# One 512-column matmul for the high weights, and weight sums made by accumulating DMAs, in a one-core streaming-encoder layer

## The chip, the cores and the metric

The kernel runs on 1 core of a Trainium2 chip. The metric is the device time of one execution in microseconds (us). Before the change three runs gave a median of 1380.38 us (1380.32 to 1382.34). The engines are named as in the profile: PE is TensorE's matmul, PEld its weight load, DVE is VectorE, ACT is ScalarE, POOL is GpSimd, and SP is SyncE, which here only issues DMAs.

## The reference

One layer over 512 positions and 2048 channels, everything in float32:

```python
hn = rmsnorm(x, norm_g)
proj = jnp.einsum('bsd,dc->bsc', hn, w_in)        # 2048 -> 6144 (q,k,v,gate of 3 branches) + 4 + 6144 merge gates
...
gates = jax.nn.sigmoid(proj[..., QKVG_COLS + N_HEADS:] + b_gate).reshape(b, s, N_BRANCH, D_MODEL)
...
ya = forgetting_attention(qa, ka, to_heads(br[:, :, 0, 2]), f_logit)
yb = chunked_relpos_attention(qb, kb, to_heads(br[:, :, 1, 2]), rel_bias)
yc = stick_breaking_attention(to_heads(br[:, :, 2, 0]), to_heads(br[:, :, 2, 1]), to_heads(br[:, :, 2, 2]))
ys = jnp.stack([from_heads(ya), from_heads(yb), from_heads(yc)], axis=2)
ys = ys * jax.nn.silu(br[:, :, :, 3])
up = jnp.einsum('bsnw,nwd->bsnd', ys, w_up)       # 512 -> 2048 for each branch
merged = jnp.sum(gates * up, axis=2)
return x + jnp.einsum('bsd,de->bse', merged, w_out)   # 2048 -> 2048
```

The two large products are the input projection and the output projection; the three attentions have four heads of 128 each.

## The kernel before, in words

**Float32 by three matmuls.** PE is fed in float32r, a rounded float32. So each operand is split into a high part and a low part: `split` lets ACT copy the source into a float32r tile (L239) and DVE subtract that from the source (L241). `mm3` (L245 to L249) adds three matmuls into one PSUM tile: high weights times high part (L247), high weights times low part (L248), low weights times high part (L249).

**Pairs by Strassen's scheme.** The positions are cut into halves of 256. Two blocks of 128 output columns, each with 2048 input channels in two halves of 1024, make one `PairTask`: a 2 by 2 product that is computed with seven block products instead of eight (in Winograd's form, with sums that are used again). One block product, a `Unit`, is 8 steps over 128 input channels, and each step is one `mm3` with 256 columns. The weights of a pair are four tiles `raw` of 128x1024 float32 (512 KB). Seven weight blocks are needed: the tiles of products 1, 2 and 4 as loaded, and four sums for products 5, 7, 6 and 3, which `sums` makes on DVE (L612, L616, L620, L625). The matching sums of the activations were made and split once (`x1`, `x2`, `t23`, `t4`, and `m...` for the output projection); a tile `Parts` holds high and low part of one half side by side, 128 x 2 x 2 x 256.

**Reading out.** A block product ends in the left 256 columns of a PSUM bank. `after_of` reads it out and adds the results up: in an ordinary pair the order of products is 1, 2, 6, 5, 7, 3, 4; products 6, 7 and 4 go on adding to the bank of product 1, and product 3 to that of product 5, so those banks are read while they are kept (ACT copies L673, L683, L689, L709; DVE adds L679, L693, L698). A pair that is built with `late=True` (two of 52: the first after the column stage, and the first of the output projection) uses another order and a fresh bank for each product, with more adds.

**What sets the order.** Everything is written as generators that a small planner (`Flow`) runs at build time. It keeps a clock for PE, ACT and DVE, gives each piece of work a cost and a due time, and writes the instructions of each engine in the order in which its model would start them. On the chip each queue then runs in that order and waits on semaphores. Weights are prepared two units ahead (`LA = 2`). Slots are counted: six `raw` tiles (`NR`), 21 tiles of 128x512 (`NT`, tag `t2`), 28 activation tiles (`NX`), and the PSUM banks of tag `acc`. Loads (`fetch`, L261) go through SP's queue, POOL has almost nothing to do.

**Stages.** Load and norm of x with the first head's columns (to about 100 us), then pairs for 11 further heads and for the merge gates with the attention of each head woven in between (to about 1078 us), then the up projections with 512-column matmuls (to about 1209 us), then eight pairs of the output projection.

Of the kernel before, what the change touches and what calls it, by code (L numbers as in the profile page):

```python
# [11 lines left out]
AF = mybir.ActivationFunctionType  # L12
# [149 lines left out]
def hybrid_kernel(  # L162
# [69 lines left out]

    def pair_of(name, dt=F32R):
        return t2(name + "h", dt), t2(name + "l", dt)
# [9 lines left out]

    def mm3(ps, lh, ll, rh, rl, start, stop, more=False):  # L245
# [3 lines left out]
        nc.tensor.matmul(ps, ll, rh, start=False, stop=stop, skip_group_check=more)  # L249

# [92 lines left out]
    class Unit:  # L343


        def __init__(self, mms, after=None, shape=(UK, P), srcs=(), room=0):
            self.shape, self.mms, self.after, self.srcs, self.room = list(shape), mms, after, srcs, room
            self.ready, self.raw, self.there = Event(), [], None

        def got(self, t, ev):  # L350
            self.raw.append((t, ev))

        def source(self):

            return self.raw[0]
# [7 lines left out]
    def load_unit(u):  # L363
        for s in u.srcs:
# [5 lines left out]
            u.got(t, fetch(to, s, flow.ready, 4 * u.shape[0] * P * P // 1024))  # L370
        for _ in range(u.room):
            yield raws, 1
            u.got(raw_tile(), None)
        if u.there is not None:
            u.there.t = 0.0

    def prep(u):
# [3 lines left out]
        if len(u.raw) < len(u.srcs) + u.room:  # L381
            u.there = Event()
            yield u.there
        src, ev = u.source()
        yield ev
        yield from split(u.hi, u.lo, src, n, u.ready)
# [105 lines left out]
    def combos(k):  # L492
# [8 lines left out]
        nc.vector.tensor_sub(a[:, LH], a[:, RH], a[:, LH])  # L501
# [3 lines left out]
        nc.vector.tensor_sub(b[:, RH], b[:, RH], a[:, LH])  # L505
        yield (DVE, q, *due)
        nc.vector.tensor_sub(b[:, LH], b[:, LH], b[:, RH])
# [20 lines left out]
    def strassen_ops(x1, x2, t23, t4):  # L528

        def part(ts, i):  # L530
            return lambda k: ts[k] and ts[k].half(i)

        return {1: part(x1, 0), 2: part(x2, 0), 3: part(x2, 1), 5: part(x1, 1), 6: part(t23, 0), 7: part(t23, 1),
                4: lambda k: t4[k // 2] and t4[k // 2].half(k % 2)}
# [28 lines left out]
    class Pair(Unit):  # L563


        def __init__(self, task, i, srcs=()):
            super().__init__(task.mms_of(i), task.after_of(i), srcs=srcs, room=1 if i == 0 else 0)
            self.task, self.p = task, task.order[i]

        def source(self):  # L570
            task = self.task
            if self.p == task.order[0]:
# [997 lines left out]
```

## Time and profile before

| what | before |
|---|---|
| median of 3 runs | 1380.38 us (1380.32 to 1382.34) |
| profiled execution | 1382.54 us, of which the span from first to last instruction is 1380.8 us |
| granted TensorE clock | 0.999 |
| DVE busy, ACT busy | 1100.3 us (80%), 772.3 us (56%) |
| data moved by DMA | 180.55 MB, mean 131 GB/s |

In the profile's groups each line gives the source line, the engine, the operation, output and inputs by the program's names, the shape and count, then busy time in us, the mean of one in ns, and the idle time of that engine just before these instructions. Matmuls overlap: one shows 280 ns, but the next starts 120 ns after it. So the pace of PE is read from the distance of two starts, not from the duration.

### The profile page before, as it was taken

The numbers are of one execution on the slowest core, as the hardware profiler recorded it, in microseconds if no ns is written. First come the engines' busy times: TensorE is split into PE (matmuls) and PEld (weight loads), VectorE is DVE, ScalarE is ACT, GpSimd is POOL, SyncE is SP. The second block draws the span as 40 slices with busy tenths as digits, with TensorE's granted clock in tenths as the row PEclk, the third lists the DMA queues.
The fourth block names the chain that finished last, engine by engine and source line by source line (L and its number), as shares of the span: only waits on it lengthen the run. The fifth ranks groups of instructions, "written<-read, shape, count | busy, mean of one in ns | idle before, by whom it ended". The sixth has DMA issues, their size and how long they took to land.

```text
span 1380.8 us, 25041 instructions
## 1 busy us (share of the span) xinstructions
PE 1363.8 (99%) x10306; PEld 1311.4 (95%) x10306; DVE 1100.3 (80%) x1488; ACT 772.3 (56%) x1233; POOL 4.4 (0%) x21
## 2 busy tenths in 40 slices
PE   7999999999999999999999999999999999989999
PEld 5789999999999999999999999999999888889998
DVE  5898987878878787787878869678687887897785
ACT  7546665646555566655667556555565755453433
POOL 0000000000000000000000000000000000000000
PEclk9999999999999999999999999999999999999999
DMA  9423333333343433434334242333425756434541
GB/s 340 152 90 111 104 100 115 96 126 121 94 123 107 131 122 94 123 113 131 116 100 123 92 143 95 108 115 108 128 80 184 278 187 193 142 94 170 177 140 63
DMA packets 68610, 180.55 MB, mean 131 GB/s; under 512 B 7672, under 2 KB 13944, under 8 KB 68496
## 3 DMA queue, kind: packets, MB, share of 16 engines
q1 hardware_dynamic: 64896, 174.69, 39.6%
q10 hardware_dynamic: 3600, 4.26, 0.9%
q8 instruction: 81, 1.33, 0.4%
q14 instruction: 33, 0.27, 0.1%
HBM read 159.24 MB, written 19.69 MB: 130 GB/s over the span
## 4 chain that ended last, share of the span: by engine, by line
PE 97%; DVE 2%; DMA 1%; issue 0%; ACT 0%; SPq 0%
PE acc L247 28%; PE acc L249 27%; PE acc L248 27%; PE att L248 3%; PE att L249 3%; PE att L247 3%; PE att L1042 1%; PE att L971 1%; DVE wl L241 1%; PE att L754 1%; PE att L1109 1%; PE att L1110 1%; PE att L1108 1%; DMA x<-in_xT 0%; PE att L1069 0%
## 5 line engine op out<-in xcount | busy, mean ns | idle before, releaser
L241 DVE TENSOR_TENSOR wl<-raw,wh 128x1024 fp32r<-128x1024 f32 (+1 forms) x412 | 493.7, 1200 | 192.1 <-ACT wh L239 191.0
L239 ACT ACTIVATE wh<-raw 128x1024 fp32r<-128x1024 f32 (+1 forms) x412 | 428.3, 1040 | 307.8 <-PE acc L248 201.1
L247 PE MATMUL acc<-x,wh 128*128 128x256 f32 (+1 forms) x1504 | 440.4, 293 | 9.1 <-ACT wh L239 9.1
L249 PE MATMUL acc<-x,wl 128*128 128x256 f32 (+1 forms) x1504 | 436.4, 290 | 0.1
L248 PE MATMUL acc<-x,wh 128*128 128x256 f32 (+1 forms) x1504 | 436.1, 290 | 0.0
L247 PEld LDWEIGHTS acc<-x,wh 128*128 128x128 f32 x1504 | 288.3, 192 | 15.4 <-ACT wh L239 9.1
L247 PE MATMUL acc<-t,wh 128*128 128x256 f32 x1056 | 301.2, 285 | 0.0
L249 PE MATMUL acc<-t,wl 128*128 128x256 f32 x1056 | 298.7, 283 | 0.0
L248 PE MATMUL acc<-t,wh 128*128 128x256 f32 x1056 | 298.7, 283 | 0.0
L248 PEld LDWEIGHTS acc<-x,wh 128*128 128x128 f32 x1504 | 288.2, 192 | 4.8 <-DVE wl L241 0.2
L249 PEld LDWEIGHTS acc<-x,wl 128*128 128x128 f32 x1504 | 287.9, 191 | 4.7 <-DVE wl L241 0.8
L247 PEld LDWEIGHTS acc<-t,wh 128*128 128x128 f32 x1056 | 202.4, 192 | 0.5
L248 PEld LDWEIGHTS acc<-t,wh 128*128 128x128 f32 x1056 | 202.4, 192 | 0.5
L249 PEld LDWEIGHTS acc<-t,wl 128*128 128x128 f32 x1056 | 202.3, 192 | 0.0
L248 PE MATMUL acc<-m,wh 128*128 128x256 f32 x448 | 127.8, 285 | 3.2 <-DVE m L241 3.2
L247 PE MATMUL acc<-m,wh 128*128 128x256 f32 x448 | 127.5, 285 | 0.8 <-ACT m L239 0.8
L249 PE MATMUL acc<-m,wl 128*128 128x256 f32 x448 | 127.6, 285 | 0.7 <-DVE wl L241 0.7
L248 PEld LDWEIGHTS acc<-m,wh 128*128 128x128 f32 x448 | 86.7, 193 | 3.8 <-DVE m L241 3.8
L247 PEld LDWEIGHTS acc<-m,wh 128*128 128x128 f32 x448 | 86.7, 194 | 1.0 <-ACT m L239 1.0
L249 PEld LDWEIGHTS acc<-m,wl 128*128 128x128 f32 x448 | 86.8, 194 | 0.9 <-DVE wl L241 0.9
L612 DVE TENSOR_TENSOR raw<-raw,raw 128x1024 f32<-128x1024 f32 x52 | 63.6, 1223 | 1.2
L625 DVE TENSOR_TENSOR raw<-raw,raw 128x1024 f32<-128x1024 f32 x52 | 63.4, 1220 | 0.6
(218 smaller groups left out, 1625.7 us busy)
## 6 DMA issues: line engine op xcount, KB each, us to landing
raw<-in_w_col SPq DMA_DIRECT2D x192, 512.0 KB, 3.6
raw<-in_w_out SPq DMA_DIRECT2D x32, 512.0 KB, 4.3
gl<-c SPq DMA_DIRECT2D x48, 256.0 KB, 2.0
raw<-in_w_up SPq DMA_DIRECT2D x32, 384.0 KB, 3.6
sg<-gl SPq DMA_DIRECT2D x48, 256.0 KB, 4.4
x<-in_xT SPq DMA_DIRECT2D x16, 256.0 KB, 6.2
xn<-in_xn SPq DMA_DIRECT2D x16, 256.0 KB, 6.2
xr<-in_xT SPq DMA_DIRECT2D x16, 256.0 KB, 4.3
```

Of the source, the lines that this page charges most:

```text
L239: nc.scalar.activation(hi, src, AF.Copy)
L241: nc.vector.tensor_sub(lo, src, f(hi))
L247: nc.tensor.matmul(ps, lh, rh, start=start, stop=False, skip_group_check=more)
L248: nc.tensor.matmul(ps, lh, rl, start=False, stop=False, skip_group_check=more)
L249: nc.tensor.matmul(ps, ll, rh, start=False, stop=stop, skip_group_check=more)
L612: nc.vector.tensor_add(w[5], w[7], w[4])
L625: nc.vector.tensor_sub(w[3], w[2], w[6])
L754: nc.tensor.matmul(two(first_ps[:2 * NH, :]), w2[:, kt, :], xs[kt].lo if j else xs[kt].hi, start=kt + j == 0, stop=kt + j == KT)
L971: nc.tensor.transpose(ps[:, blk(i)], self.p[i][:, blk(j)], identf)
L1042: nc.tensor.matmul(ps[:, i * P:], nu_r if i == j else nones_r, part, start=i == j and part is self.lk[j][0], stop=False)
L1108: nc.tensor.matmul(o, vh[:, blk(j)], h, start=j == 0, stop=False)
L1109: nc.tensor.matmul(o, vl[:, blk(j)], h, start=False, stop=False)
```

## The change

There are four parts.

- **mm2 for mm3 in the pairs.** One step of a block product becomes two matmuls: the high weights times high and low part together, 512 columns, into both halves of a PSUM bank; and the low weights times the high part, 256 columns, into the left half. The true result is the sum of the two halves.
- **Reading out.** Copies and adds now take all 512 columns, and where a result is final, `fold` adds the right half to the left. Where the sum of the blocks wants a minus sign, it folds with `minus`, which computes -a-b in one instruction. That goes with weight sums which are now plain additions: signs were moved from the weights to the activation sums (`combos`, `merged_a`, `merged_b`).
- **Weight sums.** `PairTask.load` loads five tiles instead of four; two of them (for products 5 and 7) get a second block added by an accumulating DMA that POOL issues (`add_up`), after the first one has landed. DVE makes the other two sums, in place.
- **Small ones.** `gates_of` starts its three loads together, the last product of the output pairs adds the residual in `c2_done`, and `merged_b` has a shorter due time.

```diff
+        def both(self, i):
+            return self.t[:, i, :, :], self.t[:, i, 0, :], self.ev[i]
...
+    def minus(to, a, b):
+        nc.vector.scalar_tensor_tensor(to, a, -1.0, b, op0=ALU.mult, op1=ALU.subtract)
...
+    def mm2(ps, lh, ll, r, rh, start, stop, more):
+        nc.tensor.matmul(two(ps), lh, r, start=start, stop=False, skip_group_check=more)
+        nc.tensor.matmul(ps[:, LH], ll, rh, start=False, stop=stop, skip_group_check=more)
...
+    def add_up(to, src, ready, kb):
+        nc.gpsimd.dma_start(to, src, accum_op=ALU.add)
+        line[1] = max(line[1], ready + 1.0) + kb / 170.0
+        return Event(line[1] + 2.5)
...
+        def load(self):
+            a11, a12, a21, a22 = self.src
+            for p, srcs in ((5, (a21, a22)), (1, (a11,)), (2, (a12,)), (7, (a11, a21)), (4, (a22,))):
+                yield raws, 1
+                t = self.w[p] = raw_tile()
+                ev = fetch(t, srcs[0], flow.ready, 512)
+                if len(srcs) > 1:
+                    ev = add_up(t, srcs[1], ev.t, 512)
+                self.there[p].t = ev.t
+            self.w[6], self.w[3] = self.w[1], self.w[2]
...
-            yield DVE, n
-            nc.vector.tensor_add(w[5], w[7], w[4])
-            set_(wev[5])
-            yield e1
-            yield DVE, n
-            nc.vector.tensor_sub(w[7], w[1], w[7])
-            set_(wev[7])
+            yield there[5]
             yield self.unit(1).ready
             yield DVE, n
-            nc.vector.tensor_sub(w[6], w[5], w[1])
+            nc.vector.tensor_add(w[1], w[1], w[5])
...
-            nc.vector.tensor_sub(w[3], w[2], w[6])
+            nc.vector.tensor_add(w[2], w[2], w[1])
...
-                    self.ps[p] = acc(bank)[:, LH]
+                    self.ps[p] = acc(bank)
...
-                    yield PE, mm_us(HS, 3)
-                    mm3(self.ps[p], u.hi[:, j, :], u.lo[:, j, :], rh, rl, j == 0 and not more, j == UK - 1, more)
+                    yield PE, mm_us(S) + mm_us(HS)
+                    mm2(self.ps[p], u.hi[:, j, :], u.lo[:, j, :], r, rh, j == 0 and not more, j == UK - 1, more)
...
+            def fold(to, src):
+                yield h
+                if p in (4, 7):
+                    minus(to, src[:, LH], src[:, RH])
+                else:
+                    add(to, src[:, LH], src[:, RH])
...
                 if p == 1:
+                    yield from new("u")
                     yield a
-                    nc.scalar.activation(self.u[:, LH], ps, AF.Copy)
+                    nc.scalar.activation(self.u, ps, AF.Copy)
...
                     elif p == 3:
                         yield ev[6]
                         yield v
-                        add(self.c1[:, RH], self.u[:, RH], ps)
+                        add(self.u, self.u, ps)
                         give(bank)
+                        yield from fold(self.c1[:, RH], self.u)
...
+                    else:
+                        yield lambda: hasattr(self, "c2")
+                        c = self.c2[:, LH]
+                        yield ACT, act_us(HS)
+                        nc.scalar.activation(c, ps[:, RH], AF.Copy, scale=-1.0)
+                        yield h
+                        nc.vector.tensor_sub(c, c, ps[:, LH])
                         give(bank)
```

What the change does to the order is seen at three places. On PE, in the middle of a pair, two steps of a block product stood like this before (`t` is the activation sum, `wh` and `wl` the high and low weights):

```order
L247 MATMUL acc_7720<-t_115_853,wh_7718 128x256
L248 MATMUL acc_7720<-t_115_853,wh_7718 128x256
L249 MATMUL acc_7720<-t_115_853,wl_7719 128x256
L247 MATMUL acc_7720<-t_118_870,wh_7718 128x256
L248 MATMUL acc_7720<-t_118_870,wh_7718 128x256
L249 MATMUL acc_7720<-t_118_870,wl_7719 128x256
```

and two steps with the change:

```order
L261 MATMUL acc_6473<-t_114_843,wh_6540 128x512
L262 MATMUL acc_6473<-t_114_843,wl_6541 128x256
L261 MATMUL acc_6473<-t_115_856,wh_6540 128x512
L262 MATMUL acc_6473<-t_115_856,wl_6541 128x256
```

Three rows became two; over the program PE has 2912 rows fewer, 52 pairs by 7 products by 8 steps.

On DVE, in the queue of an ordinary pair beside one head's attention, there stood before (`wl` is the low part of a weight block, `raw` a weight tile, `c` the read-out results, `al` an attention tile):

```order
L679 TENSOR_TENSOR c_6221<-c_6183,acc_6186 128x256
L241 TENSOR_TENSOR wl_6223<-raw_6174,wh_6222 128x1024
L241 TENSOR_TENSOR wl_6258<-raw_6244,wh_6257 128x1024
L241 TENSOR_TENSOR al_6256<-att_6268,ah_6255 128x512
L241 TENSOR_TENSOR wl_6298<-raw_5943,wh_6297 128x1024
L612 TENSOR_TENSOR raw_6281<-raw_6174,raw_6209 128x1024
L693 TENSOR_TENSOR c_6294<-c_6294,acc_6141 128x256
L616 TENSOR_TENSOR raw_6174<-raw_6049,raw_6174 128x1024
L241 TENSOR_TENSOR wl_6338<-raw_6049,wh_6337 128x1024
L241 TENSOR_TENSOR al_6296<-att_6308,ah_6295 128x384
L698 TENSOR_TENSOR c_6221<-c_6183,acc_6259 128x256
L620 TENSOR_TENSOR raw_6049<-raw_6281,raw_6049 128x1024
```

and at the same place of a pair with the change:

```order
L714 TENSOR_TENSOR u_5228<-u_5228,acc_5231 128x512
L690 TENSOR_TENSOR c_901_5265<-u_5228 128x256
...
L245 TENSOR_TENSOR wl_5322<-raw_5084,wh_5321 128x1024
L245 TENSOR_TENSOR al_5320<-att_5329,ah_5319 128x384
L726 TENSOR_TENSOR v_5318<-v_5318,acc_5195 128x512
L251 SCALAR_TENSOR_TENSOR c_922_5363<-v_5318 128x256
L245 TENSOR_TENSOR wl_5355<-raw_5222,wh_5354 128x1024
L245 TENSOR_TENSOR vl_5370<-att_5364,vh_5369 128x512
L633 TENSOR_TENSOR raw_5222<-raw_5222,raw_5118 128x1024
L735 TENSOR_TENSOR u_5228<-u_5228,acc_5290 128x512
```

The sums L612 and L616 are gone from the queue; each add from PSUM is twice as wide, and a fold of 256 columns stands behind it.

On SP, the loads of one pair and a bit (each row one 512 KB tile) with the change are the five in the middle of these rows:

```order
L274 DMA raw_4928<-in_w_col 128x1024
L274 DMA raw_5018<-in_w_col 128x1024
L274 DMA raw_5035<-in_w_col 128x1024
L274 DMA raw_5059<-in_w_col 128x1024
L274 DMA raw_5084<-in_w_col 128x1024
L274 DMA raw_5118<-in_w_col 128x1024
```

and POOL's queue, where no DMA stood before, has for the same tiles:

```order
L278 DMA raw_4928<-in_w_col 128x1024
L278 DMA raw_5059<-in_w_col 128x1024
L278 DMA raw_5118<-in_w_col 128x1024
```

A pair takes its tiles in the order product 5, 1, 2, 7, 4, so `raw_4928` and `raw_5059` are the accumulated tiles of one pair, and `raw_5118` is the first of the next.

More of the change, by code (lines that the diff above doesn't have):

```diff
@@ L363, in load_unit @@
     def load_unit(u):
+        if isinstance(u, Pair):
+            if u is u.task.units[0]:
+                yield from u.task.load()
+            return
         for s in u.srcs:
@@ L369, in load_unit @@
                 to = t.rearrange("p (c k) m -> p c k m", c=s.shape[1])
[L370 to L375, printed above, removed]
+            u.raw = t
+            u.there.t = fetch(to, s, flow.ready, 4 * u.shape[0] * P * P // 1024).t
     def prep(u):
@@ L380, in prep @@
         u.lo = wp.tile([P] + u.shape, F32R, tag="wl", name=nm("wl"), bufs=LA + 1)
[L381 to L386, printed above, removed]
+        yield u.source_there()
+        yield from split(u.hi, u.lo, u.source(), n, u.ready)
         u.split_done()
@@ L627, in sums, with free @@
-            yield self.unit(6).ready
+            nc.vector.tensor_add(w[2], w[2], w[1])
+            set_(there[3])
+            spawn(self.free(6), 1.0)
+        def free(self, p):
+            yield self.unit(p).ready
             give(raws)
```

166 lines of the change are left out of this document (83 added, 83 removed).

## The prediction

> **What bounds the kernel now.** I read the page's busy times, its chain that ended last, then PE's waits, then PE's starts one by one.
>
> ```profile
> span 1380.8 us, 25041 instructions
> PE 97%; DVE 2%; DMA 1%; issue 0%; ACT 0%; SPq 0%
> ...
> PE acc L247 <- ACT wh L239: 9.1, 1, 9.1
> PE acc L248 <- DVE m L241: 3.2, 3, 2.2
> PE acc L247 <- ACT m L239: 0.8, 1, 0.8
> PE acc L249 <- DVE wl L241: 0.7, 1, 0.7
> ```
>
> The chain is 97% PE. The last four rows are all of PE's waits (engine and line, what it waited for: us in total, times, longest): 9.1 us once at the start, and 4.7 us where the output projection begins. In between PE never waits. So the time is the number of matmuls by their pace, and only PE's own work, or a new wait of PE, can move it. The pace is read from starts (first column, us), where the widths meet:
>
> ```profile
> 403.67 0.28 PE L248 MATMUL acc<-x,wh 128*128 128x256 f32 x1
> 403.79 0.28 PE L249 MATMUL acc<-x,wl 128*128 128x256 f32 x1
> 403.91 0.40 PE L869 MATMUL att<-sqh,ones_r 128*128 128x512 f32 x1
> 404.14 0.39 PE L870 MATMUL att<-sql,ones_r 128*128 128x512 f32 x1
> 404.37 0.28 PE L247 MATMUL acc<-x,wh 128*128 128x256 f32 x1
> 404.49 0.28 PE L248 MATMUL acc<-x,wh 128*128 128x256 f32 x1
> ...
> 1109.66 0.39 PE L248 MATMUL att<-y,wh 128*128 128x512 f32 x1
> ...
> 1111.02 0.39 PE L248 MATMUL acc<-y,wh 128*128 128x512 f32 x1
> ```
>
> 256 columns take 0.12 us (403.67, 403.79, 403.91; 404.37, 404.49). 512 columns take 0.2267 us: from 1109.66 to 1111.02 there are six, 1.36 / 6. Twice the columns cost 0.1067 us more, so each matmul pays 0.2267 - 2 x 0.1067 = 0.0133 us whatever its width. The rows at 403.79 to 404.49 show that a change of width costs nothing on top, neither from 256 to 512 nor back: each has the distance of its own width.
>
> **The change part by part: PE.** A step was three matmuls of 256, 0.360 us. It becomes one of 512 and one of 256, 0.2267 + 0.1200 = 0.3467 us. The columns streamed are the same; one fixed part of 0.0133 us is saved. There are 52 pairs x 7 products x 8 steps = 2912 steps, and the two orders differ by that many PE rows: 2912 x 0.01333 = 38.8 us off the path.
>
> The Trainium skill, "TensorE: Matmul & The Clock Gate", section "Back-to-back issue gap", has the gap of single matmuls at N/2.4 + 2.5 ns when warm, and says that this leaves out the weight load. By its 2.5 ns the 2912 matmuls would be worth an estimated 7.3 us; the 13.3 ns of the rows, where every matmul loads weights, says 38.8.
>
> **Reading out and weight sums.** Durations by shape, from DVE's and ACT's groups (last columns: busy us, mean ns):
>
> ```profile
> L612 DVE TENSOR_TENSOR raw<-raw,raw 128x1024 f32<-128x1024 f32 x52 | 63.6, 1223 | 1.2
> L1342 DVE TENSOR_TENSOR sg<-att,sg 128x512 f32<-128x512 f32 x32 | 22.0, 687 | 13.0 <-PE att L249 13.0
> L698 DVE TENSOR_TENSOR c<-c,acc 128x256 f32<-128x256 f32 x50 | 20.8, 415 | 2.8 <-PE acc L249 2.2
> L441 DVE SCALAR_TENSOR_TENSOR rs<-rw,rt 128x512 f32<-128x512 f32 x16 | 11.1, 692 | 0.6
> ...
> L673 ACT ACTIVATE c<-acc 128x256 f32<-128x256 f32 x52 | 19.8, 381 | 29.0 <-PE acc L249 24.4 <-DMA out<-c 3.7
> L239 ACT ACTIVATE vh<-att 128x512 fp32r<-128x512 f32 x12 | 7.0, 582 | 0.0
> ```
>
> An ordinary pair on DVE: before, four sums of 1.22 and three adds of 0.415, 6.13 us. After, two sums, three adds of 512 columns at 0.687, and four steps of 256 (three folds, and one subtraction for product 4) at 0.42, 6.18 us. The instruction that `minus` uses has no price of its own: at 512 columns it takes 692 ns in L441, as a plain tensor-tensor does, so I take it as equal. ACT: before four copies of 0.38, 1.53 us; after three of 0.58 and one of 0.38, 2.13 us. So DVE stays even, and ACT gets 0.6 us per pair. Whether that hides is seen in the stretch of pairs:
>
> ```profile
> 200.00:1000.00 800.00, 800.00 (x6580) 794.79 (x6579) 631.33 (x799) 459.86 (x730) 1.57 (x3) 1.00 0.37 114
> ...
> L247 PE MATMUL acc<-x,wh 128*128 128x256 f32 x1172 | 334.3, 285 | 0.0
> L239 ACT ACTIVATE wh<-raw 128x1024 fp32r<-128x1024 f32 x256 | 270.3, 1056 | 158.6 <-PE acc L248 144.8 <-DVE raw L620 9.3 <-issue 4.4
> L247 PE MATMUL acc<-t,wh 128*128 128x256 f32 x873 | 248.9, 285 | 0.0
> ...
> 100.00:200.00 100.00, 100.00 (x788) 97.98 (x787) 89.07 (x146) 60.29 (x105) 0.00 (x0) 1.00 0.32 101
> 130.00:140.00 10.00, 10.00 (x82) 9.87 (x82) 9.80 (x18) 7.53 (x13) 0.00 (x0) 1.00 0.42 132
> ```
>
> The rows with a colon are window, length, then busy PE, PEld, DVE, ACT, POOL, then clock, DMA share and GB/s. In 800 us PE is busy throughout; (1172 + 873) / 56 = 36.5 pairs make 21.9 us a pair, with DVE 17.3 and ACT 12.6 us. With the change a pair lasts 21.9 - 0.75 = 21.17 us, with DVE 17.35 (82% for 79%) and ACT 13.2 us (62% for 57%). Between 130 and 140 us DVE is busy 98% and PE loses nothing: weights prepared two units ahead bridge it. So I cost this at nothing. Its cover is one product: where a product adds on to a bank that is still to be read out (6 on 1, 7 on 6, 3 on 5, 4 on 7), exactly one other product, 8 x 0.3467 = 2.77 us, stands between. The read-out takes 0.58 on ACT or 0.69 on DVE, and may stand behind a weight instruction of 1.06 (L239) or 1.22 us (L612's shape): 1.6 to 1.9 us. If that cover fails, PE waits, and the weights behind it in the two queues get late next.
>
> **The accumulating DMAs.** Nothing in the trace accumulates, so the cost is bounded by plain loads.
>
> ```profile
> raw<-in_w_col SPq DMA_DIRECT2D x192, 512.0 KB, 3.6
> q1 hardware_dynamic: 64896, 174.69, 39.6%
> ```
>
> A 512 KB load lands 3.6 us after its issue. By the stretch above, where 114 GB/s keep the 16 engines busy for 37%, 0.524 MB use 4.6 x 0.37 = 1.70 us of all sixteen (the whole program's 174.69 MB at 39.6% say 1.64). A pair has 8.1 us of such DMA time now. It gets one plain load more, 1.7, and two accumulates. The lower end is a plain load each, 1.7, in all 13.2 of 21.17 us (62%). The upper end is where the engines are full: (21.17 - 9.8) / 2 = 5.7 us each, 3.3 times a load. I take twice, 3.4 us each, as an accumulate also has to read the tile that it adds to: 78%. Latency is covered better still: with six slots a pair's tile for product 7 gets its slot when the pair before has split its own, one whole pair ahead, so 21 us for a load of 3.6 and the accumulate, and that for product 5 more. On SP the fifth load stands before the next pair's; SP waits there for slots that DVE frees, not for POOL. POOL's rows wait only for the first load and the slot. Three memsets of `forget_sums` stand among them in POOL's queue, and the planner puts these where their tiles come free. So nothing on the path; from 5.7 us on each further microsecond costs 104 of them.
>
> **Start of the output projection and end.** PE's waits on `m` there (3.2 us, L241) stand in DVE's queue behind this:
>
> ```profile
> 1199.57 1.22 DVE L612 TENSOR_TENSOR raw<-raw,raw 128x1024 f32<-128x1024 f32 x1
> 1201.36 1.22 DVE L616 TENSOR_TENSOR raw<-raw,raw 128x1024 f32<-128x1024 f32 x1
> ...
> 1377.60 0.42 DVE L705 TENSOR_TENSOR c<-xr,acc 128x256 f32<-128x256 f32 x1 [1.73 <-PE acc L249]
> ```
>
> Two sums of 1.22 us leave the queue just ahead of the splits that PE waits for, so up to 2.4 us come back; wider adds of the late pair (0.27 each) take some of it. I take 2.0, with bounds of 3.2 (all that wait) and 0. At the end one DVE instruction (L705) lay between the last matmul and the last store. With the change it is an ACT copy of 0.38, a subtraction and an add of 0.42 each: 0.8 us more, with no cover.
>
> **The sum.** The profiled execution took 1382.5 us for its span of 1380.8. 1382.5 - 38.8 - 2.0 + 0.8 = 1342.5. The median of the three runs is 2.2 us below that execution, so 1340.3. The hot stretch between 100 and 200 us, where DVE is 89% busy, holds the other late pair: seven adds that are 0.27 us wider and four folds of 0.42, against two sums of 1.22 less, 1.1 us more. It may cost a wait of that size at most, and I add most of it: 1341.
>
> **The rivals.**
>
> *The read-out becomes a wait.* If each pair loses once what ACT's and DVE's read-out have grown by together (0.2 + 0.27, say 0.4 us), 52 x 0.4 = 21 us come back: 1362. For it: DVE's share rises to 82%, and the extra tiles `u`, `v` at full width take `t2` slots for longer. Against it: no wait today in 1000 us, with 2.77 us of cover.
>
> *The accumulates fill the DMA engines: slower.* At four times a plain load, 6.8 us each, a pair needs 8.1 + 1.7 + 13.6 = 23.4 us of DMA time for 21.17 us of PE. PE then waits 2.2 us per pair for product 5's or 7's weights, 52 x 2.2 = 116 us: 1457. It decides from 3.3 times on, and makes the kernel slower from 3.6 times (0.75 us per pair). For it: nothing here shows how fast the engines add. Against it: 37% busy now, 21 us of lead.
>
> *The fixed part is not saved.* If a step of 512 and 256 cost nearly its old 0.360 us, because the 13.3 ns belonged to the columns or the load of weights and not to the instruction, only the page's 2.5 ns a matmul would be left: 1380.4 - 7.3 - 1.2 = 1372. Against it stand the starts at 403.79 to 404.49.
>
> **How the numbers follow.** The forecast, 1336 to 1348, gets 0.67; read-out waits (1348 to 1376) 0.20; the unsaved fixed part 0.03; DMA engines full 0.10. The range runs from 1336 (all 4.7 us of waits gone at the start of the output projection, no wait in the hot stretch, and 2 us for the spread between runs) to 1365, which takes in about three quarters of the read-out rival: 0.67 + 0.15 = 0.82. A difference under 0.2%, 2.8 us, can't be told from no change. Faster by more than that: the forecast, read-out waits and the unsaved fixed part, less 0.02 for waits that happen to eat it all: 0.88. Within it 0.02. Slower 0.10.
>
> **What would show it.** PE: some 7394 matmuls instead of 10306, starts in a pair 0.227 and 0.120 us apart, and PE's list of waits still without any on `u`, `v` or `raw` between 100 and 1070 us. DVE near 1104 us busy, ACT near 806 (34 more). DMA's share in the stretch of pairs about 0.78; POOL's DMAs landing in 4 to 8 us. The prediction is wrong if a step takes 0.36 us, if PE waits for an ACT or DVE read-out once per pair, or if the accumulates take over 5.7 us of the DMA engines each.

## The result, and the profile after

The median fell from 1380.35 us (4 runs, 1380.07 to 1382.34) to 1358.22 us (4 runs, 1357.42 to 1359.96): a ratio of 0.9838, 95% interval 0.9821 to 0.9855. The change saves 22 us, where 39 were forecast. The direction was right. The time lies inside the stated range, 1336 to 1365, but outside the forecast's own part of it, 1336 to 1348: the point, 1341, is 17 us too low.

The page of the changed kernel, its DMA queues, PE's list of waits, and the stretch of pairs between 200 and 1000 us (columns as in the prediction):

```profile
span 1356.7 us, 19802 instructions
PE 1336.8 (99%) x7394; PEld 1154.0 (85%) x7394; DVE 1106.6 (82%) x1592; ACT 803.6 (59%) x1240; POOL 94.2 (7%) x125
...
q0 software_dynamic: 14976, 54.53, 23.9%
...
raw<-in_w_col SPq DMA_DIRECT2D x236, 512.0 KB, 4.2
raw<-in_w_col POOLq DMA_DIRECT2D x88, 512.0 KB, 6.3
```

```profile
PE acc L255 <- ACT wh L243: 9.9, 1, 9.9
PE acc L261 <- DVE m L245: 4.0, 1, 4.0
PE att L256 <- DVE y L245: 1.0, 1, 1.0
PE acc L262 <- DVE wl L245: 0.8, 2, 0.5
```

```profile
200.00:1000.00 800.00, 800.00 (x4641) 700.80 (x4640) 651.24 (x890) 492.00 (x747) 65.42 (x77) 1.00 0.71 189
```

The number of matmuls, DVE's and ACT's busy time and the DMA share are near what was forecast (7394 matmuls, 1104 and 806 us, and a share of 0.78, where 0.71 was measured). PE is busy all 800 us and never waits there for a read-out or a sum. So what is missing in this stretch is missing in PE's own pace. Its starts, in the stretch of pairs:

```profile
499.36 0.40 PE L261 MATMUL acc<-x,wh 128*128 128x512 f32 x1
499.59 0.28 PE L262 MATMUL acc<-x,wl 128*128 128x256 f32 x1
499.71 0.40 PE L261 MATMUL acc<-x,wh 128*128 128x512 f32 x1
499.95 0.28 PE L262 MATMUL acc<-x,wl 128*128 128x256 f32 x1
...
502.19 0.40 PE L261 MATMUL acc<-x,wh 128*128 128x512 f32 x1
```

From 499.36 to 502.19 lie eight steps: 2.83 / 8 = 0.354 us, not 0.3467. The mean over all steps of pairs without an interruption (2464 steps; starts of the trace, gaps of over 25 ns left out) is 233.9 ns for 512 and 116.6 for 256, 350.6 together. By stages, each from the start of its first matmul to that of the next stage's:

| stage | before | after | difference | forecast |
|---|---|---|---|---|
| pairs up to the up projection | 969.9 | 947.5 | -22.3 | -32.0 (with the hot stretch) |
| up projection | 130.6 | 132.3 | +1.7 | 0 |
| first pair of the output projection | 26.6 | 27.5 | +0.9 | -2.75 |
| its seven other pairs | 142.0 | 137.0 | -5.0 | -5.2 |
| last matmul to the end | 3.55 | 4.31 | +0.8 | +0.8 |

Three rows are short: pairs by 9.7, the up projection by 1.7, the start of the output projection by 3.6. The other 2 us of the 17 are the step from the profiled execution to the median: it was 2.2 us before, and is 0.2 now.

### The profile page after: what moved, and what is told of

Same layout as the page of the kernel before. It is cut to its first block, busy times and chain, and to the rows that moved or that the text cites. A ratio compares the mean times of both kernels' runs of the same rounds, so it can differ in the third digit from the quotient of the medians.

```text
span 1356.7 us, 19802 instructions
## 1 busy us (share of the span) xinstructions
PE 1336.8 (99%) x7394; PEld 1154.0 (85%) x7394; DVE 1106.6 (82%) x1592; ACT 803.6 (59%) x1240; POOL 94.2 (7%) x125
## 3 DMA queue, kind: packets, MB, share of 16 engines
q0 software_dynamic: 14976, 54.53, 23.9%
## 4 chain that ended last, share of the span: by engine, by line
PE 96%; DVE 2%; DMA 1%; ACT 0%; issue 0%; SPq 0%; ACTq 0%; DVEq 0%
PE acc L261 49%; PE acc L262 25%; PE att L256 3%; PE att L257 3%; PE att L255 3%; PE acc L257 3%; PE acc L256 3%; PE acc L255 3%; DVE wl L245 1%; PE att L1088 1%; PE att L1017 1%; PE att L1156 1%; PE att L1155 1%; PE att L800 1%; DVE m L245 1%; PE att L1154 1%
## 5 line engine op out<-in xcount | busy, mean ns | idle before, releaser
L261 PE MATMUL acc<-x,wh 128*128 128x512 f32 x1408 | 505.8, 398 | 0.0
L262 PE MATMUL acc<-x,wl 128*128 128x256 f32 x1408 | 394.1, 280 | 0.0
L261 PE MATMUL acc<-t,wh 128*128 128x512 f32 x1056 | 381.0, 398 | 0.0
L261 PEld LDWEIGHTS acc<-x,wh 128*128 128x128 f32 x1408 | 264.5, 188 | 60.9
L261 PEld LDWEIGHTS acc<-t,wh 128*128 128x128 f32 x1056 | 198.4, 188 | 45.3
L261 PE MATMUL acc<-m,wh 128*128 128x512 f32 x448 | 158.8, 397 | 4.0 <-DVE m L245 4.0
L278 POOL DMA_DIRECT2D raw<-in_w_col x88 | 76.1, 864 | 943.1 <-DMA raw<-in_w_col 515.5
L261 PEld LDWEIGHTS acc<-m,wh 128*128 128x128 f32 x448 | 85.1, 190 | 23.6 <-DVE m L245 4.3
L722 ACT ACTIVATE u<-acc 128x512 f32<-128x512 f32 x50 | 29.8, 596 | 56.9 <-PE acc L262 56.9
L699 ACT ACTIVATE u<-acc 128x512 f32<-128x512 f32 x52 | 30.9, 593 | 41.0 <-PE acc L262 37.1
L256 PE MATMUL att<-y,wh 128*128 128x512 f32 x128 | 50.0, 391 | 1.1 <-DVE y L245 1.0
```

What stands on the lines that cost most here:

```text
L256: nc.tensor.matmul(ps, lh, rl, start=False, stop=False, skip_group_check=more)
L261: nc.tensor.matmul(two(ps), lh, r, start=start, stop=False, skip_group_check=more)
L262: nc.tensor.matmul(ps[:, LH], ll, rh, start=False, stop=stop, skip_group_check=more)
L278: nc.gpsimd.dma_start(to, src, accum_op=ALU.add)
L699: nc.scalar.activation(self.u, ps, AF.Copy)
```

## The experiments

Eleven kernels ran, in three lots. Ratios are to the kernel before, run beside them (1380.17, 1380.38 and 1380.59 us in the three lots).

**Which part is worth what: the merged matmul taken apart.**

```diff
-        nc.tensor.matmul(two(ps), lh, r, start=start, stop=False, skip_group_check=more)
+        nc.tensor.matmul(ps[:, LH], lh, rh, start=start, stop=False, skip_group_check=more)
+        nc.tensor.matmul(ps[:, RH], lh, r[:, 1, :], start=False, stop=False, skip_group_check=more)
```

> The wide read-out, the accumulating DMAs and everything else of the change, but the 512-column matmul taken apart again into two of 256 (high weights times high part into the left half, times low part into the right half). It measures what the merged matmul alone is worth. Theory A: PE's starts are 0.120 apart throughout as before, a step 0.360, so 2912 x (0.360 - 0.3503) = 28 us more than the changed kernel: 1386, that is some 6 us above the kernel before, the price of the other parts (start of the output projection, end). Theory B (DMA traffic slows PE): starts in the pairs over 0.120, step over 0.363, 1395 or more. If the other parts of the change bring nothing and cost nothing: 1380.

Measured: 1382.72 us, ratio 1.0019 (1.0009 to 1.0028). Its steps are 120 ns per matmul again. So all the other parts together, wide read-outs, folds and accumulating DMAs, cost 2.5 us (1382.72 - 1380.17), and the merged matmul alone brings 24.5 us (1382.72 - 1358.22): 8.4 ns per step, not 13.3. So most of the missing part belongs to the merged matmul, not to its surroundings.

**Do the accumulating DMAs slow PE down?** The 104 accumulating DMAs were left out, so the weights of products 5 and 7 lack their second tile.

```diff
-                if len(srcs) > 1:
-                    ev = add_up(t, srcs[1], ev.t, 512)
```

> The changed kernel without its 104 accumulating DMAs: the second block of the weight sums for products 5 and 7 is left out, so the output is not the reference's; loads, DVE, ACT and PE are as in the changed kernel. Theory A: PE's pace in the pairs is unchanged (0.350 per step), 1357 to 1358. Theory B: the pace returns to 0.3467 and the time to 1348. If the accumulates delay the start of the output projection or the up projections, one to three us come back there and nothing in the pairs.

Measured: 1359.58 us, ratio 0.9844 (0.983 to 0.9859), the same as the change. The stretch of pairs:

```profile
200.00:1000.00 800.00, 800.00 (x4639) 700.67 (x4638) 651.26 (x890) 492.18 (x747) 1.57 (x3) 1.00 0.46 140
```

4639 matmuls in 800 us for 4641: not one is bought by leaving them out, although the DMA share falls from 0.71 to 0.46. So contention of the DMAs with PE is out. The fall also prices the accumulate: 0.25 x 800 / 74 = 2.7 us of all sixteen engines each (77 of POOL's instructions less three memsets); by the queue's share it is 0.239 x 1356.7 / 104 = 3.1.

**The order of widths: grouped and folded.** In the first kernel a product does eight matmuls of 512, then eight of 256; in the second the order inside every other step is turned round, 512, 256, 256, 512.

```diff
-                    yield PE, mm_us(S) + mm_us(HS)
-                    mm2(self.ps[p], u.hi[:, j, :], u.lo[:, j, :], r, rh, j == 0 and not more, j == UK - 1, more)
+                    yield PE, mm_us(S)
+                    nc.tensor.matmul(two(self.ps[p]), u.hi[:, j, :], r, start=j == 0 and not more, stop=False,
+                                     skip_group_check=more)
+                for j in range(UK):
+                    r, rh, ev = self.ops[p](j)
+                    yield PE, mm_us(HS)
+                    nc.tensor.matmul(self.ps[p][:, LH], u.lo[:, j, :], rh, start=False, stop=j == UK - 1,
+                                     skip_group_check=more)
```

```diff
-                    mm2(self.ps[p], u.hi[:, j, :], u.lo[:, j, :], r, rh, j == 0 and not more, j == UK - 1, more)
+                    for i in ((0, 1) if j % 2 == 0 else (1, 0)):
+                        if i == 0:
+                            nc.tensor.matmul(two(self.ps[p]), u.hi[:, j, :], r, start=j == 0 and not more,
+                                             stop=j == UK - 1, skip_group_check=more)
+                        else:
+                            nc.tensor.matmul(self.ps[p][:, LH], u.lo[:, j, :], rh, start=False, stop=False,
+                                             skip_group_check=more)
```

> Each block product issues its eight 512-column matmuls first and then its eight 256-column ones; the same matmuls, columns and DMAs, but two changes of width per product instead of sixteen. Theory A (the lost part of the gain is the price of alternating widths: in the changed kernel a 512 is followed by a 256 after 0.230 to 0.241 us and that by a 512 after 0.112 to 0.120, 0.3503 us per step in the mean where 0.3467 was expected, some 10 us over the pairs): 512s 0.227 apart, 256s 0.120 apart, the stretch from the first pair to the first up projection 937 us instead of 947.5, total 1348. Theory B (the accumulating DMAs and the higher DMA traffic slow PE's reads): no change, 1358. Theory C (waits for the read-out of PSUM): no change or a little worse, 1358 to 1362.

> Steps in the order 512, 256, 256, 512, 512, 256, 256, 512: half the changes of width. Theory A by dose: half of the 10 us comes back, 1353. If the loss hangs on the rhythm of one 512 and one 256 and not on the number of changes, all of it comes back, 1348. Theories B and C: 1358.

Measured: grouped 1356.15 us (0.9824, 0.9808 to 0.9841), folded 1352.55 us (0.9797, 0.9782 to 0.9812). A step of pairs takes 349.5 and 348.7 ns, for 350.6 in the change. The order of widths matters, with the same instructions; but rows of eight of one width still don't reach 346.7. Within its rows of eight, the grouped kernel's 512s were 230 to 231 ns apart on average, where the up projection has 226.7. One difference was left that could explain it: a pair's operand of 512 is one run of 512 numbers, the up projection reads two runs of 256.

**The operand's layout.** The tiles of the pair operands were laid out as the up projection's, and in a second kernel the up projection's as the pairs' were.

```diff
-            self.hi, self.lo = self.t[:, :, 0, :], self.t[:, :, 1, :]
+            self.v = self.t if apart else self.t.rearrange("p h l s -> p l h s")
+            self.hi, self.lo = self.v[:, 0, :, :], self.v[:, 1, :, :]
...
-            return self.t[:, i, :, :], self.t[:, i, 0, :], self.ev[i]
+            return self.v[:, :, i, :], self.v[:, 0, i, :], self.ev[i]
```

> The tiles of pair operands are laid out with all high halves ahead of all low halves, so that the 512-column operand of a step is two runs of 256 numbers, as the up projection's was before; the y tiles keep their old layout, and the column sums, which read a high or a low half of a whole row, now read 512 numbers in one run. Theory of the operand's layout (512 numbers in one run take 231 to 235 ns, two runs of 256 take 226.7): a step falls from 350.5 to 346.7 ns, 2912 x 3.8 = 11 us less in the pairs, and the column sums' 416 or so matmuls get 4.3 ns each more, 1.8 us: 1349, with 512 followed by 256 at 227 ns. Theory of the alternation (the price comes from a change between 512 and 256, whatever is read): nothing in the pairs, +1.8 in the column sums: 1358 to 1360, with 512 followed by 256 still at 234 ns.

> The run before with the same layout for the y tiles as well, so that the up projection's 576 matmuls of 512 read one run of 512 numbers, where they read two runs of 256. There is no change of width in that stage, so only the layout can tell. Theory of the layout: each takes 4.3 to 8 ns more, the stage 2.5 to 4.6 us, so 1351.5 to 1353.5 if the run before gives 1349; starts 231 to 235 ns apart there. Theory of the alternation: the stage is as before, 226.7 ns, and the two runs take the same.

Measured: 1359.69 us (0.9851, 0.9834 to 0.9867) and 1358.39 us (0.9842, 0.9828 to 0.9857), both as the change. The pairs' step is 350.6 ns in both, as in the change, and the up projection's 512s are 226.8 apart in either layout. The theory of the layout falls. It had rested on comparing stages that differ in a second thing as well: in the up projection nothing but 512s follow each other.

**Settling after a change of width.** So the grouped kernel's rows were sorted by place: the first 512 after 256s is followed after 233.3 ns (mean of 376), the next ones after 234.8, 229.5, 232.0 and 230.2, and from the sixth on after 226.7. Among the 256s the first is short, 114.3, then 119.1 and 119.7 to 120. A row needs about five matmuls to reach the pace of its own width. That gives two numbers to try: rows of four should gain nothing, and rows of sixteen should gain more than rows of eight. In the lists below `k` is 1 for a 512 and 0 for a 256, and `j` is the step. The first has rows of four; in the second, products 6, 7 and 4 begin with their 256s, so that rows of two products join to sixteen.

```diff
...
+                seq = [(k, 4 * q + j) for q in range(2) for k in (1, 0) for j in range(4)]
...
```

```diff
...
+                seq = [(k, j) for k in ((0, 1) if p in (6, 7, 4) else (1, 0)) for j in range(UK)]
+                if self.late:
+                    seq = [(k, j) for j in range(UK) for k in (1, 0)]
...
```

> Each product's eight steps as four matmuls of 512, four of 256, four of 512, four of 256: four changes of width per product, where the change has sixteen and the grouped run two. Theory of settling: a matmul of 512 keeps its 226.7 ns only from the sixth in a row on; in the grouped run the first five after a change are 233.3, 234.8, 229.5, 232.0 and 230.2 ns apart, and the first 256s 114.3, 119.1, 119.7 and 119.9. Of each row of four only the unsettled ones are left, 2 x (929.6 + 473.0) / 8 = 350.65 ns a step where the grouped run has 349.0: some 4.8 us slower than the grouped run, no better than the change, 1357 to 1361. Theory of a fixed price per change of width (the change's 30 ns over sixteen): four changes cost 8 ns per product, 347.6 ns a step, 1346 to 1352.

> Eight matmuls of 512 and eight of 256 per product as in the grouped run, but products 6, 7 and 4 of the ordinary pairs begin with their 256s, so that at three of four borders of products the width doesn't change: 4 rises to 512 and 4 falls per pair, where the grouped run has 7 of each; the late pairs keep the change's order. Theory of settling: a rise costs 26.3 ns and a fall gives back 8, so 4 x 18.3 = 73 ns per pair against 128 in the grouped run and 213 in the change: 50 x 0.14 = 7.0 us less than the change, 1350 to 1353. Theory of a price per change: 50 x 7 x 30.4 = 10.6 us less 50 x 8 x 1.9 = 0.8: 1347 to 1349. If the low weights, now wanted 1.85 us earlier, come late: waits of PE on VectorE's splits, and nothing gained.

Measured: rows of four 1358.54 us (0.9838, 0.9824 to 0.9853), rows of up to sixteen 1352.90 us (0.9796, 0.978 to 0.9812). Both lie where settling had them, 1357 to 1361 and 1350 to 1353, and outside what a fixed price per change would give. PE's starts in the second kernel, each row a run of equal matmuls:

```profile
502.72 2.00 PE L666 MATMUL acc<-t,wh 128*128 128x512 f32 x8
504.56 1.98 PE L666 MATMUL acc<-x,wh 128*128 128x512 f32 x8
506.37 1.12 PE L668 MATMUL acc<-x,wl 128*128 128x256 f32 x8
507.32 1.12 PE L668 MATMUL acc<-t,wl 128*128 128x256 f32 x8
508.28 0.86 PE L666 MATMUL acc<-t,wh 128*128 128x512 f32 x3
```

The first eight 512s take 1.84 us, 230 ns each; the eight behind them 1.81, 226. The 256s give a little back: 0.95 us, then 0.96. And in rows of four:

```profile
503.29 1.09 PE L666 MATMUL acc<-t,wh 128*128 128x512 f32 x4
504.22 0.64 PE L668 MATMUL acc<-t,wl 128*128 128x256 f32 x4
504.70 1.09 PE L666 MATMUL acc<-t,wh 128*128 128x512 f32 x4
```

0.93 us for four 512s, 232.5 ns each, and 1.41 us for four steps, 352 here and 350.6 on average.

What settling doesn't explain is the order of single steps. Folded rows have only two matmuls of a width each time, and by the numbers above should take as long as the change; they take 2 ns less. The change's own steps show why one number isn't enough. The output projection has the same instructions in the change and in the kernel with both layouts altered but for where its operands lie. Its steps there, first those of the change:

```profile
1299.81 0.39 PE L261 MATMUL acc<-m,wh 128*128 128x512 f32 x1
...
1302.58 0.39 PE L261 MATMUL acc<-m,wh 128*128 128x512 f32 x1
```

then those of the kernel with both layouts:

```profile
1299.81 0.40 PE L261 MATMUL acc<-m,wh 128*128 128x512 f32 x1
...
1302.64 0.40 PE L261 MATMUL acc<-m,wh 128*128 128x512 f32 x1
```

Eight steps take 2.77 us (346 ns) in one execution and 2.83 us (354 ns) in the other. Over the stage the means are 347.8 and 353.2 ns; the kernel without the accumulating DMAs has the change's layout and 352.9. So it isn't the layout either: an alternation of 512 and 256 falls into one of two rhythms and keeps it until something interrupts it, in the change's output projection for 342 steps. Over the 448 steps of that stage the two differ by 2.4 us, as much as the whole spread of the change's runs.

The same two rhythms make up the 350.6 ns of the pairs. In the trace of the change the 57 uninterrupted steps from 462.1 us take 346.8 ns each, the 67 from 486.3 us, among them the eight shown at the start, 353.1. Of 206 groups of eight steps in the pairs, 81 take 346 to 348 ns a step and 125 take 351 to 354. The faster rhythm is the 346.7 that was forecast; there the two widths alternate and nothing is paid on top. All 122 uninterrupted runs of steps in the pairs have the same length and the same pace (to 0.5 ns) in both layout kernels, and 92 of them in the kernel without the accumulating DMAs. So it isn't chance of the execution, and what PE has done just before seems to pick the rhythm; what about it does so wasn't tried.

**What the accumulating DMAs are worth.** The merged matmul and the wide read-outs stay, but all four sums of a pair are on DVE again, from four plain loads.

```diff
-            for p, srcs in ((5, (a21, a22)), (1, (a11,)), (2, (a12,)), (7, (a11, a21)), (4, (a22,))):
+            for p, src in ((1, a11), (7, a21), (4, a22), (2, a12), (5, None)):
...
+            nc.vector.tensor_add(w[5], w[7], w[4])
...
+            nc.vector.tensor_add(w[7], w[1], w[7])
```

> The change with its 512-column matmuls and wide read-outs, but all four weight sums of a pair on VectorE again and no accumulating DMA. VectorE gets two sums of 1.22 us per pair more, 17.35 + 2.44 = 19.8 of 21.3 us, 93%. If VectorE's relief was needed for the gain: PE gets waits on VectorE's work in the stretch of pairs, 10 to 50 us in all, 1368 to 1400. If it was not: 1356 to 1361 as the change.

Measured: 1458.13 us, ratio 1.0562 (1.0546 to 1.0578): 100 us slower than the change, where waits of 10 to 50 us were expected, and 78 us slower than before. PE's waits, and the stretch of pairs:

```profile
PE acc L262 <- DVE wl L245: 60.9, 29, 4.0
PE acc L261 <- DVE m L245: 7.4, 2, 3.8
```

```profile
200.00:1000.00 800.00, 763.28 (x4342) 662.74 (x4342) 685.74 (x914) 463.08 (x695) 1.57 (x3) 0.99 0.34 109
```

PE waits 29 times for low weights, and PE's busy time grew by 33 us as well (1370.1 for 1336.8), mostly because after such waits it runs at half rate for a while (below; the granted clock is 0.979 on average, for 0.997 in the change). DVE's queue ahead of one of these waits:

```profile
519.30 1.22 DVE L636 TENSOR_TENSOR raw<-raw,raw 128x1024 f32<-128x1024 f32 x1
520.44 1.22 DVE L245 TENSOR_TENSOR wl<-raw,wh 128x1024 fp32r<-128x1024 f32 x1
...
523.23 1.22 DVE L640 TENSOR_TENSOR raw<-raw,raw 128x1024 f32<-128x1024 f32 x1
524.37 0.42 DVE L757 TENSOR_TENSOR c<-c,acc 128x256 f32<-128x256 f32 x1
524.70 1.22 DVE L245 TENSOR_TENSOR wl<-raw,wh 128x1024 fp32r<-128x1024 f32 x1
525.83 1.22 DVE L644 TENSOR_TENSOR raw<-raw,raw 128x1024 f32<-128x1024 f32 x1
526.97 0.69 DVE L454 SCALAR_TENSOR_TENSOR rs<-rw,rt 128x512 f32<-128x512 f32 x1
527.57 1.22 DVE L650 TENSOR_TENSOR raw<-raw,raw 128x1024 f32<-128x1024 f32 x1
...
530.90 1.22 DVE L245 TENSOR_TENSOR wl<-raw,wh 128x1024 fp32r<-128x1024 f32 x1
```

```profile
532.17 0.39 PE L262 MATMUL acc<-t,wl 128*128 128x256 f32 x1 [2.41 <-DVE wl L245]
```

All four sums stand within 10 us, among the splits and the read-outs, without a gap, and the split that began at 530.90 ends where PE goes on, at 532.17. Over the pair DVE has room (86% busy in the window); in these ten microseconds it has none.

A third of the loss, 34 us, arises in the output projection, where no attention shares DVE. There each pair behind the first takes 23.3 to 23.9 us for 19.4. DVE is busy 73% of the time (17.5 us of the 24 from 1348 on). It idles 4.7 us in one piece before 1346.10, but from 1348.87 on it works without a gap through all four sums of a pair, and PE waits 2.3 us for the split behind them.

But four sums close together are not the whole cause, for the kernel before had them too. Here are its first and last sum of a pair:

```profile
608.35 1.22 DVE L612 TENSOR_TENSOR raw<-raw,raw 128x1024 f32<-128x1024 f32 x1
...
616.00 1.22 DVE L625 TENSOR_TENSOR raw<-raw,raw 128x1024 f32<-128x1024 f32 x1
```

They lie within 9 us, also without a gap, and PE didn't wait. There a read-out between them was one add of 0.42 us; here it is mostly an add of 0.68 and a fold of 0.42, and PE asks for its weights sooner (a product of eight steps takes 2.8 us for 2.88). That these together are what tips it is argued, not shown.

**Half of that load.** To the change one DVE instruction per pair was added that alters nothing, as long as a sum and just ahead of one:

```diff
+            nc.vector.tensor_tensor(w[5], w[5], w[5], op=ALU.max)
             nc.vector.tensor_add(w[1], w[1], w[5])
```

> The change, with one VectorE instruction more per pair that alters no number (the larger of product 5's weights and themselves, 128x1024, 1.22 us), put ahead of the sum for product 6 without the planner knowing of it. VectorE gets 18.57 of 21.3 us per pair, 87%; the run with all four sums on VectorE has two such instructions more and loses 100 us. Theory of load (PE waits in proportion to what VectorE has over its 82%): some 50 us, 1400 to 1415. Theory of a threshold (the planner's lead of two units absorbs the first microseconds): 1358 to 1365.

Measured: 1366.44 us, ratio 0.9893 (0.9878 to 0.9907), 8 us more than the change. Its stretch of pairs:

```profile
200.00:1000.00 800.00, 799.90 (x4639) 700.42 (x4638) 689.99 (x929) 491.23 (x746) 66.29 (x78) 1.00 0.72 189
```

DVE is as busy as with the four sums, 690 us of 800 for 686, and PE loses 0.1 us. (PE got further in that time, 4639 matmuls for 4342, so per pair DVE still has less to do here.) The result lies just above what the theory of a threshold allowed, 1365, and far below that of load, 1400. Of the 6.7 us between the two spans 2.1 arise before the up projection (a wait of 0.8 us near 140 us, in the hot stretch, is one of them), 1.6 in the second pair of the output projection, 1.9 in the five behind it because their steps have the slower rhythm, and 1.2 in the last. So a loss in proportion to the load is out as the cause of the 100 us. A limit of DVE's load between this kernel and the one with four sums is not, and how much of the 100 us the place of the two sums makes, and how much their number, was not separated. What the accumulating DMAs bought is room on DVE.

**The start of the output projection.** Here PE waits 4.0 us on `m`. One more kernel (on the first altered layout) let the planner put the last merges earlier:

```diff
-                    spawn(merged_b(d - UK, m[0]), 4.0, flow.fin)
+                    spawn(merged_b(d - UK, m[0]), 1.5, flow.fin)
```

> As the layout run, with the last pairs' merge put earlier in the planner's order (slack 1.5 for 4.0), so that VectorE's subtractions for m and its splits stand some ten rows earlier in its queue. If the 4.0 us wait of PE on m at the start of the output projection, and the matmuls at half rate behind it (8 x 0.2 = 1.6 us), come from the place of these in VectorE's queue: the wait falls to 1 us or less and the clock stays at 1.00, 3 to 5 us off the layout run, 1344 to 1346 if that gives 1349. If they come from the last products' sums themselves, which no place in a queue makes earlier: within 1 us of the layout run.

Measured: 1359.12 us (0.9843, 0.9827 to 0.986), within 1 us of the layout run's 1359.69: no gain. PE's waits after the first:

```profile
PE acc L262 <- DVE wl L245: 5.1, 2, 4.9
PE att L256 <- DVE y L245: 1.0, 1, 1.0
```

The wait on `m` is gone, and one of 4.9 us on low weights stands in its place. What is put ahead in DVE's queue there puts something else behind it.

## Why the prediction was right, and where its sizes were wrong

**The number of steps and their cover: right.** The forecast said that PE alone bounds the kernel, that fewer matmuls make it faster, and that read-out and accumulates hide. 2912 matmuls left, the stretch of pairs stayed free of waits, and the read-out had its cover. Reading out even on DVE and 0.6 us more per pair on ACT came out at 1106.6 and 803.6 us busy. The accumulates, taken at 3.4 us of the DMA engines each, measured 2.7 to 3.1, within the bounds of 1.7 and 5.7, and taking them away moved nothing. But "DVE stays even" carried more than the text said: with the two sums still on DVE the kernel was 78 us slower than before. The prediction named DVE's 82% as a risk for the read-out, and didn't ask what the same wide read-outs would cost without the accumulates.

**The price of a step: mis-sized.** The term 2912 x 0.01333 = 38.8 us used 0.2267 for the 512, from the up projection, and "a change of width costs nothing on top". That sentence failed as a rule: it holds in the faster rhythm, 346.7 ns a step, and not in the slower one, about 353, in which the pairs spent more than half of their steps. The rows quoted for it couldn't carry it. From 403.91 to 404.37 two matmuls of 512 take 0.46 us where 2 x 0.2267 = 0.453, and a time rounded to 0.01 us can't tell these apart; to the nanosecond the trace has 235 and 231. The mean of the 44 pairs of such rows in the trace of before is 234 ns. Measured by the trace, the change's step took 350.6 ns in the pairs and 347.8 in the output projection: 2464 x 3.9 + 448 x 1.1 = 10.1 us less than the term promised.

The Trainium skill, "TensorE: Matmul & The Clock Gate", section "Back-to-back issue gap", would have made the 2912 matmuls worth 2.5 ns each, an estimated 7.3 us. The merged matmul alone brought 24.5 us, 8.4 ns each. The rows were the better guide, though not as exact as they were taken for.

**The start of the output projection: wrong.** The prediction gave back 2.0 us there because two sums leave DVE's queue. They left, and PE still waited 4.0 us in one piece, with a second price behind it. DVE and ACT just before PE goes on at 1206.88:

```profile
1201.98 1.76 DVE L245 TENSOR_TENSOR m<-mu,m 128x256 fp32r<-128x256 f32 x5
1203.66 0.42 DVE L251 SCALAR_TENSOR_TENSOR mt<-mt,sg 128x256 f32<-128x256 f32 x1
...
1206.13 0.68 DVE L245 TENSOR_TENSOR m<-mt,m 128x512 fp32r<-128x512 f32 x1
```

```profile
1204.11 0.63 ACT L243 ACTIVATE m<-mt 128x512 fp32r<-128x512 f32 x1 [3.44 <-DVE mt L251]
```

The last `m` that PE needs goes from DVE (L251) to ACT and back to DVE, and the L251 stands behind five other splits; ACT sat idle 3.44 us for it. Back on DVE it stands behind 1.4 us of other work once more. The step that failed priced an edit by the instructions that leave the queue, and not by the order in which the planner writes the rest. With the wide adds the late pair's read-out grew as well; what that made of the wait wasn't measured. What follows the wait is PE at half rate, 0.43 us for a 512 and 0.21 for a 256:

```profile
1207.47 0.41 PE L262 MATMUL acc<-m,wl 128*128 128x256 f32 x1
1207.68 0.63 PE L261 MATMUL acc<-m,wh 128*128 128x512 f32 x1
1208.11 0.41 PE L262 MATMUL acc<-m,wl 128*128 128x256 f32 x1
...
1212.54 0.28 PE L262 MATMUL acc<-m,wl 128*128 128x256 f32 x1
```

Eight steps from 1207.47 to 1212.54 take 5.07 us, where eight others take 2.8: 2.3 us on top of the 4.0. In the kernel before, the 4.7 us of waits lay in five pieces of at most 2.2 us, and behind the longest 15 matmuls of 256 came 213 ns apart instead of 120, 1.4 us more. The first row is PE's longest wait there, the second the window around it, with a clock of 0.76:

```profile
1220.34 0.47 PE L248 MATMUL acc<-m,wh 128*128 128x256 f32 x1 [2.21 <-DVE m L241]
```

```profile
1217.00:1224.00 7.00, 4.79 (x28) 4.59 (x27) 7.00 (x14) 2.82 (x7) 0.00 (x0) 0.76 0.52 150
```

So the two starts cost about the same: by PE's starts, the first two pairs of the stage took 7.4 us more than two of its later pairs then (20.16 us each), and 8.2 us more now (19.41 each). The sums that left the queue bought nothing.

**Smaller terms.** The end came out as worked out (+0.8). The up projection's 1.7 us were not forecast; 1.0 of them is a wait on `y`, which the trace of before doesn't have. The rival of a read-out wait was near in its time, 1362, but not in its cause: the waits it asked for are not there. The range reached to 1365 only to take in most of that rival, so that it holds the measured time is luck; the mechanism was right, and two terms of the sum were too large.

## What to carry to other kernels

Read a pace from the sum over many starts in the very pattern that the new kernel will have; distances of single rows rounded to 0.01 us hide 3%, and a row of equal matmuls in another stage is another pattern. Where two widths must follow each other, put equal widths together in long rows: grouping in sixteens, with the same instructions, was worth 5 us more than the change (1352.9 us, 2.0% under the kernel before), and so was turning every other step round. And when an edit widens work on an engine, look at its fullest ten microseconds and not only at its share: in the stretch of pairs DVE was 86% busy both in the kernel with four sums, where PE waited, and in the one with a single instruction more than the change, where PE lost nothing.

## What the runs showed of the hardware

- The distance between matmuls depends on those before them. In rows of eight, the first two 512s behind 256s take 233 to 235 ns, the next three 229.5 to 232, and 226.7 comes only from the sixth on; the first 256 behind 512s takes 114 ns, then 119 to 120. An alternation of single matmuls runs in one of two rhythms, about 346.7 or 353.4 ns a step with the same instructions, once for 342 steps.
- Whether 512 numbers lie in one run or in two of 256 makes no difference to a matmul: 226.8 ns in both.
- A wait of PE can cost more than its length. In the kernel with all sums on DVE, windows around three waits:

```profile
438.00:444.00 6.00, 3.59 (x16) 2.85 (x15) 5.23 (x8) 1.69 (x2) 0.00 (x0) 0.85 0.57 170
529.00:535.00 6.00, 3.59 (x21) 2.86 (x20) 5.50 (x8) 1.90 (x3) 0.00 (x0) 1.00 0.49 158
506.00:512.00 6.00, 4.33 (x24) 3.40 (x23) 5.90 (x8) 4.98 (x9) 0.00 (x0) 1.00 0.50 159
```

The first two hold a wait of the same 2.41 us; behind the first the granted clock falls (0.85 over the window, 16 matmuls for 21), behind the second it doesn't. The third holds one of 1.67 us. In that trace the distance of two starts is 11 times 1.8 to 1.9 us over the usual one, never followed by half rate, and 16 times 2.5 to 2.9 us over it, 13 times followed by it. The Trainium skill, "TensorE: Matmul & The Clock Gate", section "What's actually happening", puts the fall to half rate after one idle window of about 3.4 us, and says that the windows run freely. That a break of one length does it at one time and not at another agrees with free-running windows; that 2.4 us of waiting (2.6 with the time around it) suffice, and in the trace of before even a wait of 2.2, does not agree with a whole idle window of 3.4.
- A 512 KB accumulating DMA took 2.7 to 3.1 us of all sixteen DMA engines, landed 6.3 us after its issue (plain loads 4.2), and cost PE nothing.
